# Other homes for the output gates and other prices for side work in a one-core fp32 decoder layer

## The chip, the cores and the metric

The kernel is one program on one core of a Trainium2 chip. The metric is the device time of one execution in microseconds (us), as the median over several. The engines in the profile are PE (TensorE matmuls), PEld (its weight loads, which overlap), DVE (VectorE), ACT (ScalarE), POOL (GpSimd) and SP (which starts most transfers).

## The reference, cut to what matters

One layer of a hybrid decoder for 256 prompt tokens and 8 sample tokens (264 columns), width 2048, all in fp32. Everything of the first part comes out of one projection of the normalized input:

```python
z = rmsnorm(x, g_mix) @ w_in
xr, conv_new = causal_conv(z[RGX], conv_buf, conv_w, conv_b)      # RG-LRU, 1024 channels
log_a = -8 * sigmoid(block_diag(xr, w_rg_a)) * softplus(-lam)
a = exp(log_a); bx = sqrt(1 - exp(2 * log_a)) * (sigmoid(block_diag(xr, w_rg_x)) * xr)
h_rg = scan(h = a * h + bx)
y_rg = rmsnorm(h_rg * gelu(z[RGG]), g_rg_out)
h_ml, C, n, m = mlstm(z[Q], z[K], z[V], z[I], log_sigmoid(z[F]), C0, n0, m0)   # 4 heads
y_ml = rmsnorm_per_head(h_ml, g_ml_out) * sigmoid(z[O])           # 1024 channels
x = x + concat(y_rg, y_ml) @ w_out
x = x + cross_attention(rmsnorm(x, g_xa), memory) ; x = x + swiglu(rmsnorm(x, g_ffn))
return rmsnorm(x, g_final), all new states
```

The change lies in all that comes up to `w_out`, and in the norm of the memory tokens (`mem_gen`) that is done beside it. The cross attention, the SwiGLU layer and the final norm are as they were.

## The kernel before, in words

**Steps.** Activations lie transposed, channels on the 128 partitions and 264 tokens in a row. A projection is cut into blocks of 128 output channels, and each block is a *step*, an entry of the list `steps`, with index `i`. An fp32 product is made of three matmuls on fp32r parts (`mm3`): high x high, high x low, low x high. A step has 16 chunks of 128 input channels, so 48 matmuls, and it has two halves of 8 chunks, 24 matmuls each, because its weights come in two pieces of 128 x 1024.

A piece is loaded into a `raw` buffer (5 of them) by a transfer from SP, and is split into a `w` buffer (4 of them) by `split_half`: ScalarE copies the high part to fp32r, VectorE subtracts it to get the low part. A `w` buffer comes free when the half step that reads it has ended. The right operands lie in `B` buffers (26) as pairs of high and low parts. Results go to PSUM banks, `mm` for steps (4) and `ax` for all else (4).

The steps in order: 0 to 3 are the RG-LRU input blocks 0 to 3, done together chunk by chunk in four banks (`pe_first`), with pieces that are split in parts as `x` arrives; 4 to 7 are the blocks 4 to 7 of it; 8 the input and forget gates (`pe_if`); 9 to 16 q and k; 17 to 24 v; 25 to 32 the RG-LRU output gates (`rgg`); 33 to 40 the mLSTM output gates (`evac_o`); 41 to 56 the output projection `w_out`, whose right operand `ry(c)` is y_rg for chunks 0 to 7 and y_ml for 8 to 15; then the queries, keys and values of the cross attention, and so on.

**The norm of x.** Steps 0 to 40 use x times the gain, without the norm. The factor `rstd` of each token is multiplied in when a result is taken out of PSUM. `norm_x` makes it: sums of squares `acc_x` (one ScalarE square and one VectorE sum per chunk), column sums by matmul, an rsqrt of 12 small VectorE operations on 128x3 columns (`c`), and `spread`, three matmuls that lay the columns out over all partitions. Until it is done no step's result leaves PSUM.

**Side work.** What is not a step is written as Python generators: `norm_x`, `rg_gen` (exponentials, roots and scans of the RG-LRU), `ml_prompt` and `ml_sample` (the mLSTM; in the second the sample states `B` are scaled by `bcs` and multiplied into `nums`), `ml_norm` (per head: squares and sums into a B buffer, four matmuls with `pick`, an rsqrt on 128x12 columns, four spreads, eight products), `mem_gen` (squares and sums over the memory tokens in `lt`, then the norm). After each step the loop calls `pump`, which lets them run on in order of their priority while two virtual clocks, one for VectorE and one for ScalarE, are behind the virtual clock of TensorE. The clocks advance by the prices of `price_dve`, `price_act` and `price_pe`. `finish` runs side work without regard to the clocks until a condition holds; a step's `need` names generators that must be finished before it.

The results of a step wait in `pend` and are taken out at the next step, at high priority. `rg_gen` must be done before step 25 (`need=("rg",)`). `evac_o(j)` takes out an output gate, and makes the product with the mLSTM output at once; for that it calls `finish` until `ml_norm` has that head (`ml["nn"]`), so the whole of `ml_norm` is forced at step 33's evacuation.

The order that comes out of the Python is not the order on the engines: a scheduler of the language orders each engine's instructions by a time model and by priority. `in_order()` and `manual_schedule` keep the written order for the named engines within them.

The main loop's lines that the text speaks of:

```python
        if i == 5:
            finish(lambda: fn.done)
            st["rg"] = side(rg_gen(), 0)
        for q in need:
            if q in st:
                finish(lambda: st[q].done)
```

Of the kernel before, what the change touches and what calls it, by code (L numbers as in the profile page):

```python
# [17 lines left out]
P = 128  # L18
D = 2048
KC = D // P  # L20
T = 256
# [40 lines left out]


def price_dve(name, n, a, k):
# [3 lines left out]
    return 0.07 + n * (0.00052 if fast else 0.0066 if name == "reciprocal" else 0.00104)  # L68


def price_act(name, n, a, k):
    return 0.12 + n * 0.00083

# [7 lines left out]
def layer_kernel(ctx: ExitStack, tc, xT, memT, vec, wrg, w_in, w_out, w_q, w_k, w_v, w_o,  # L81
# [120 lines left out]
    def split_first(i, h):  # L202
# [9 lines left out]
        splits[i, h] = (wh, wl)  # L212

    def wrows(w, i):

        w = w[:, WO: WO + 8 * N].rearrange("p (c n) -> p c n", n=N)
        return w[:, :, 0: P], w[:, :, P: 2 * P]
# [97 lines left out]

    warm(12)
    onesr = const.tile([P, P], F32R, name="onesr")
# [294 lines left out]
    def evac_if(ps):  # L612
        R = Arr(7)
        ml["R"] = R
        li, u, a, b = (R(j)[0:4] for j in range(4))
        act.activation(halves(a), unturn(ps[64:68, :N]), AF.Copy)
        act.activation(halves(b), unturn(ps[96:100, :N]), AF.Copy)
        dve.tensor_add(halves(li), unturn(ps[0:4, :N]), halves(a))
        dve.tensor_add(halves(u), unturn(ps[32:36, :N]), halves(b))
        dve.tensor_mul(li, li, rstd[0:4, :])  # L620
        dve.tensor_mul(u, u, rstd[0:4, :])
        dve.tensor_scalar(li, li, V("bi")[0:4], None, op0=OP.add)
        dve.tensor_scalar(u, u, V("bf")[0:4], None, op0=OP.add)
        ml["gates"] = side(ml_gates(), 1)
# [6 lines left out]
    def ml_gates():  # L631
# [32 lines left out]
        for h in range(H):  # L664
            pe.matmul(ps[:, h * 16: h * 16 + 16], ident[0:4, h: h + 1].to_broadcast([4, P]), x16,
                      start=True, stop=True)
        i4 = ident[0:4, 0:4]
        for j in range(2):
            pe.transpose(ps[:, 64 + 4 * j: 68 + 4 * j], g[:, j * P: j * P + P], i4)
        for j, w0 in enumerate(WIN):  # L670
            pe.transpose(ps[:, 72 + 4 * j: 76 + 4 * j], b[:, w0: w0 + P], i4)
        act.activation(bcs, ps[:, 0:64].rearrange("p (h j) -> p h j", j=16), AF.Copy)
# [30 lines left out]
    def ml_prompt():  # L703
# [11 lines left out]
        R = ml["R"]  # L715
        M = R(6)[0:4, :T]
        for h in range(H):
            sel = ident[0:4, h: h + 1].to_broadcast([4, P])
            bc = bank("ax")
# [138 lines left out]
    def ml_norm():  # L858
# [35 lines left out]
        for h in range(H):  # L894
# [112 lines left out]
    def mem_gen():  # L1007
# [14 lines left out]
        for c in range(KC):  # L1022
# [3 lines left out]
            split(m[:, :T], m[:, T:], x, V("g_mem", c))  # L1026
            yield 0.7

    def ry(c):
# [304 lines left out]

    load_x(sp, 0, 1)
    for c in range(4):
        load_first(0, c)
    for i in range(1, 3):
        for c in range(0, 4, 2):
# [3 lines left out]
        if i == 1:  # L1343
            sp.dma_start(vecs[:, 16:], vec[:, 16:])
    with tc.high_priority(), in_order():
        act.dma_start(vecs[:, 0:16], vec[:, 0:16])
        load_x(act, 1, 2)
        load_x(act, 2, 4)
        act.activation(warm_act, ones[:, 0:1], AF.Square)
        split_half(0, 0)  # L1350
        split_half(0, 1)

    pend = []
    for i, (src, cols, pef, evf, need) in enumerate(steps):
# [19 lines left out]
        if 1 <= i < 4:  # L1374
            with tc.issue_after(st["split"].ins):
                for c in range(4 * i if i > 1 else 0, 4 * i + 4):
                    sumsq(acc_x, xres[:, c, :], c == 0)
        if i == 3:
            fn = side(norm_x(), -1)
        if evf is not None:  # L1380
# [9 lines left out]
        if i == 24:  # L1390
            ml["ng"] = side(ml_norm(), 6)
        if i == 40:
# [114 lines left out]
```

## Time and profile before

| | |
|---|---|
| median of 3 runs | 1467.48 us (1466.98 to 1468.0) |
| profiled execution, its own time | 1467.75 us |
| its span | 1466.0 us |
| PE busy | 1446.3 us (99%) |
| DVE busy | 1063.4 us (73%) |
| ACT busy | 783.8 us (53%) |
| POOL busy | 126.1 us (9%) |
| moved by transfers | 326.01 MB, mean 222 GB/s |
| mean granted TensorE clock | 0.995 |

The span is what the profile covers; the execution's own time is 1.75 us longer. All recorded instructions are made by one helper, so nearly every row names L60, and an instruction is told by its tiles: `w<-raw` is the split of a weight piece, `mm<-B,w` a step's matmul, `ax<-...` one of the side work. In timelines and groups the buffers' numbers are left out. A timeline row has start, length, engine, line, operation, out<-in, shapes, count, and in brackets the idle time ahead of it with what ended it. A row of a table of stretches has the stretch, its length, the busy time and count of PE, PEld, DVE, ACT and POOL, then the granted clock as a share of full speed, the share of the transfer engines and GB/s. A row of a group has, behind the bar, busy time and mean nanoseconds, and behind the second bar the idle time ahead of its instructions and what ended most of it.

### The profile page before, as it was taken

The page shows a single profiled execution, that of the slowest core. Times are in us where ns is not written, and L with a number is a line of the kernel's source. Part 1 is how long each engine was busy: PE and PEld are TensorE (multiplying, and loading weights), DVE is VectorE, ACT ScalarE, POOL GpSimd, SP SyncE. Part 2 cuts the span into 40 slices and gives each one's busy share as a digit, 9 for nine tenths or more (in the row PEclk, how much of TensorE's full clock was granted, in tenths as well). Part 3 has the DMA queues.
Part 4 walks back from the last instruction along what each step waited for, and adds up shares of the span by engine and source line. Part 5 has one row for each costly group of instructions (what it writes and reads, how often), then busy time and mean ns, then how long its engine had stood idle before and what let it go on. Part 6 is the DMA issues. An engine that isn't in the chain of part 4 may idle for free.

```text
span 1466.0 us, 30118 instructions
## 1 busy us (share of the span) xinstructions
PE 1446.3 (99%) x12052; PEld 1418.9 (97%) x12052; DVE 1063.4 (73%) x2050; ACT 783.8 (53%) x1254; POOL 126.1 (9%) x193
## 2 busy tenths in 40 slices
PE   8999999999999999999999999999999999999997
PEld 8998899999999999999999999999999999999997
DVE  7986888898799999986676656555566555566564
ACT  7565675675466666665544444344444434444463
POOL 0001110000124344320000000000000000000000
PEclk9999999999999999999999999999999999999999
DMA  9554986556799989955655555655555565555563
GB/s 280 206 187 156 309 300 230 186 189 216 246 364 335 341 280 343 346 201 186 198 192 194 194 198 193 199 192 197 196 193 201 189 200 193 196 196 193 173 193 111
DMA packets 99756, 326.01 MB, mean 222 GB/s; under 512 B 10944, under 2 KB 19824, under 8 KB 99616
## 3 DMA queue, kind: packets, MB, share of 16 engines
q1 hardware_dynamic: 83472, 269.57, 54.8%
q0 software_dynamic: 15136, 53.16, 10.1%
q8 instruction: 94, 1.54, 0.4%
q10 hardware_dynamic: 1008, 1.36, 0.3%
q14 instruction: 46, 0.38, 0.1%
HBM read 312.78 MB, written 11.28 MB: 221 GB/s over the span
## 4 chain that ended last, share of the span: by engine, by line
PE 51%; issue 42%; DVE 3%; DMA 2%; ACT 2%; POOL 0%; POOLq 0%; SPq 0%; DVEq 0%; ACTq 0%
PE mm L60 48%; PE ax L60 4%; DVE B L60 2%; DVE w L60 1%; DMA raw<-w_in 1%; ACT B L60 1%; ACT w L60 0%; DMA B<-scr 0%; DMA o_sc<-B 0%; ACT L60 0%; DMA scr<-lt 0%; DVE acc_x L60 0%; POOL B L1399 0%; ACT t L60 0%; POOL B L830 0%
## 5 line engine op out<-in xcount | busy, mean ns | idle before, releaser
L60 PE MATMUL mm<-B,w 128*128 128x264 f32 (+1 forms) x10960 | 1286.6, 279 | 7.4 <-ACT w L60 2.8
L60 PEld LDWEIGHTS mm<-B,w 128*128 128x128 f32 x10960 | 1264.8, 190 | 18.1 <-DVE w L60 3.5
L60 DVE TENSOR_TENSOR w<-raw,w 128x1024 fp32r<-128x1024 f32 (+1 forms) x522 | 624.4, 1198 | 300.5 <-ACT w L60 299.5
L60 ACT ACTIVATE w<-raw 128x1024 fp32r<-128x1024 f32 (+1 forms) x522 | 536.3, 1029 | 549.9 <-PE mm L60 383.0
L60 PE MATMUL mm<-w,B 128*128 128x512 f32 x384 | 86.5, 380 | 0.0
L60 PEld LDWEIGHTS mm<-w,B 128*128 128x128 f32 x384 | 70.7, 189 | 9.4
L1399 POOL TENSOR_TENSOR B<-B,rstd 128x264 f32<-128x264 f32 x4 | 2.8, 740 | 803.4 <-ACT rstd L60 803.4
L60 DVE TENSOR_TENSOR t<-mm,rstd 128x264 f32<-128x264 f32 x104 | 44.8, 431 | 28.4 <-PE mm L60 28.3
L60 DVE SCALAR_TENSOR_TENSOR B<-B,dw 128x256 f32<-128x256 f32 x128 | 53.7, 473 | 2.8 <-ACT dw L60 2.6
L60 DVE TENSOR_TENSOR xres<-xres,mm 128x264 f32<-128x264 f32 (+1 forms) x81 | 34.3, 424 | 27.6 <-PE mm L60 27.5
L60 DVE SCALAR_TENSOR_TENSOR dw<-B,qsm,dw 128x256 f32<-128x256 f32 x96 | 48.7, 512 | 0.8
L60 PE MATMUL ax<-B,B 128*128 128x256 f32 (+3 forms) x288 | 47.2, 305 | 0.8 <-DVE B L60 0.7
L1083 POOL TENSOR_TENSOR ds<-dw,ds 128x256 fp32r<-128x256 f32 x32 | 36.0, 1126 | 105.2 <-ACT ds L60 105.1
L60 PEld LDWEIGHTS ax<-B,B 128*128 128x128 f32 x288 | 39.5, 191 | 4.5 <-DVE B L60 1.4
L60 ACT ACTIVATE B<-xres,vecs 128x264 fp32r<-128x264 f32 (+1 forms) x64 | 32.1, 502 | 4.8 <-DVE xres L60 4.0
L60 ACT ACTIVATE t<-xres 128x264 f32<-128x264 f32 (+1 forms) x61 | 23.9, 409 | 15.9 <-DVE xres L60 15.9
L1072 POOL DMA_DIRECT2D B<-kcT x32 | 17.3, 542 | 142.4 <-DVE B L60 129.5
L60 ACT ACTIVATE dw<-B,qsm 128x256 f32<-128x256 f32 x32 | 16.3, 509 | 19.9 <-issue 9.9
L60 DVE SCALAR_TENSOR_TENSOR B<-xres,vecs,B 128x264 fp32r<-128x264 f32 x48 | 23.4, 488 | 3.5 <-ACT B L60 3.5
L60 DVE TENSOR_TENSOR acc_x<-acc_x,t 128x264 f32<-128x264 f32 x59 | 25.1, 426 | 1.0 <-ACT t L60 0.5
L60 ACT ACTIVATE t<-t 128x264 f32<-128x264 f32 (+1 forms) x61 | 24.7, 406 | 1.5 <-DVE t L60 1.5
L60 ACT ACTIVATE B<-t 128x264 fp32r<-128x264 f32 (+1 forms) x60 | 24.1, 409 | 1.5 <-DVE t L60 1.5
(168 smaller groups left out, 673.3 us busy)
## 6 DMA issues: line engine op xcount, KB each, us to landing
raw<-w_gu SPq DMA_DIRECT2D x176, 512.0 KB, 3.9
raw<-w_d SPq DMA_DIRECT2D x80, 512.0 KB, 4.2
raw<-w_in SPq DMA_DIRECT2D x74, 512.0 KB, 4.7
raw<-w_out SPq DMA_DIRECT2D x32, 512.0 KB, 4.5
B<-kcT POOLq DMA_DIRECT2D x32, 512.0 KB, 9.3
raw<-w_q SPq DMA_DIRECT2D x32, 512.0 KB, 5.1
B<-vcT POOLq DMA_DIRECT2D x32, 512.0 KB, 10.8
raw<-w_k SPq DMA_DIRECT2D x32, 512.0 KB, 5.3
```

Source lines behind the costliest of these rows:

```text
L60: return f(*a, **k)
L1072: pool_e.dma_start(kc, kcT[h, b])
L1083: pool_e.tensor_sub(ws[:, 1], acc, ws[:, 0].bitcast(F32))
L1399: e.tensor_mul(st["y"](c), st["y"](c), r)
```

## The change

1. *Start.* 8 warm-up matmuls instead of 12; the first weight piece is the first transfer of SP, the first chunk of x goes to ScalarE's queue, the next three behind weight pieces on SP.
2. *Squares.* In step 1 those of chunks 0 to 7 are made one by one, as before. Chunks 8 to 15 are done at step 3 by two squares of 128x1056 and four sums (`last_squares`), in place of eight of each.
3. *First norm.* `norm_x` is no longer forced at step 5. PE's order is as written in steps 4 to 6, and the two parts of `norm_x` are written into it: the column sums in step 5 after chunk 8, the spread in step 6 after chunk 2. The results of steps 3 to 6 leave PSUM from step 7 on, and `rg_gen` begins at 7 instead of 5.
4. *Prices.* `price_dve` and `price_act` have higher fixed parts and rates for some kinds (the scan twice the rate) until step 41; from there on they are the old ones.
5. *Output gates.* `evac_o` makes the sigmoid and leaves it in a B array `z`. `ml_norm`, written on by a loop over eight blocks, multiplies and splits. `ml_norm` has to be done before step 41 (`need` "ng"), and nothing asks for it before. Step 40's results leave PSUM ahead of that.
6. *Gate rows.* Two tiles of the gates are zeroed on GpSimd, and the matmuls that select and transpose gate rows use all 128 rows in place of 4.
7. `mem_gen`'s last loop gives way every second chunk.

The diff, cut:

```diff
 def price_dve(name, n, a, k):
...
+    rate = {"reciprocal": 0.0066, "tensor_tensor_scan": 0.00208}.get(name, 0.00052 if fast else 0.00104)
+    fixed = 0.21 if name == "scalar_tensor_tensor" else 0.15
+    return fixed + n * rate + (0.08 if "accum_out" in k else 0.0)
 def price_act(name, n, a, k):
...
+    return (0.27 if by_column else 0.18) + n * 0.00085 + (0.2 if "accum_out" in k else 0.0)
+    def last_squares():
+        a, b = (B([P, BW])[:, 0: 4 * N] for _ in range(2))
+        for t, q in ((a, 2), (b, 3)):
+            act.activation(t, xres[:, 4 * q: 4 * q + 4, :].rearrange("p c n -> p (c n)"), AF.Square)
+        dve.tensor_add(a, a, b)
...
+        dve.tensor_add(acc_x, acc_x, a[:, 0: N])
-    warm(12)
+    warm(8)
     def evac_if(ps):
+        for q in range(2):
+            pool_e.memset(R.tile(q), 0.0)
     def ml_norm():
...
-            ml["nn"] = h + 1
+        for j in range(8):
+            while ml.get("zn", 0) <= j:
+                yield STEP
+            if j == 0:
+                st["yml"] = HL(8)
+            z = ml["z"](j)
+            dve.tensor_mul(z, z, hh(j))
+            split(*st["yml"](j), z, V("g_ml", j))
+            yield 0.8
     def evac_o(j):
         def f(ps):
-            z = tmp()
+            if j == 0:
+                ml["z"] = Arr(8)
+            z = ml["z"](j)
             dve.tensor_mul(halves(z), unturn(ps[:, :N]), halves(rstd))
             act.activation(z, z, AF.Sigmoid)
-            if j == 0:
-                st["yml"] = HL(8)
-            finish(lambda: ml.get("nn", 0) > j // 2)
-            dve.tensor_mul(z, z, hT["t"](j))
-            split(*st["yml"](j), z, V("g_ml", j))
+            ml["zn"] = j + 1
     def proj(src, rhs, evac, cols=2048, n=N, need=()):
+                if (i, c) in ((5, 9), (6, 3)):
+                    with tc.high_priority():
+                        st["rstd_x"].run(lambda: True)
     for m in range(KC):
         proj(w_out[m], ry, residual(m, "g_xa", "xa", norm_wide),
-             need=("rgout",) if m == 0 else ())
+             need=("rgout", "ng") if m == 0 else ())
...
-        if i == 5:
-            finish(lambda: fn.done)
+        if i == 7:
             st["rg"] = side(rg_gen(), 0)
+        if "ng" in need:
+            with tc.high_priority(300):
+                for e, x in pend:
+                    e(x)
+            pend = []
-        if i != 4:
+        if not 4 <= i < 7:
+        if i == 4:
+            kept.enter_context(tc.manual_schedule(engines={mybir.EngineType.PE}))
         ps = pef(i)
+        if i == 6:
+            kept.close()
-            ml["ng"] = side(ml_norm(), 6)
+            st["ng"] = side(ml_norm(), 6)
+        if i == 41:
+            PACE["full"] = False
```

**Where the instructions stand.** In the rows that follow a name's first number tells apart tiles of one kind, and `x2` says that two alike stand together.

TensorE before, in step 33's and 34's x projections (`mm_383`, `mm_396`): `ax_378` is the bank into which `ml_norm` sums its squares with `pick`.

```order
L60 MATMUL mm_383_2987<-B_37_360,w_374_2913 128x264
L60 MATMUL ax_378_2969<-B_358_2810,pick_91 4x264
L60 MATMUL mm_383_2987<-B_36_359,w_374_2913 128x264
L60 MATMUL ax_378_2969<-B_358_2810,pick_91 4x264
L60 MATMUL mm_383_2987<-B_36_359,w_374_2913 128x264
L60 MATMUL ax_378_2969<-B_358_2810,pick_91 4x264
L60 MATMUL mm_383_2987<-B_37_360,w_374_2913 128x264
...
L60 MATMUL mm_396_3080<-B_13_150,w_381_2981 128x264
L60 MATMUL mm_396_3080<-B_14_151,w_381_2981 128x264
L60 MATMUL ax_378_2969<-B_358_2810,pick_91 4x264
```

TensorE after, at the output projection: `mm_489`, `mm_496`, `mm_502` and `mm_508` are the banks of steps 41 to 44, `w_494` and `w_500` the first pieces of 43 and 44, `w_391`, `w_488`, `w_495` and `w_501` the second pieces of 41 to 44, `B_359` and `B_371` parts of y_rg, `B_471` of y_ml. Of the `w` buffers one is `w_494`, then `w_500`, then `w_501`.

```order
L60 MATMUL mm_502_3936<-B_371_3250,w_494_3865 128x264
L60 MATMUL mm_508_4001<-B_359_3114,w_500_3930 128x264
...
L60 MATMUL mm_508_4001<-B_371_3250,w_500_3930 128x264
L60 MATMUL ax_443_3637<-B_433_3602,pick_87 4x264 x4
...
L60 MATMUL ax_467_3717<-ident_69,c_447_3649 128x128 x2
...
L60 MATMUL mm_489_3806<-B_471_3742,w_391_3412 128x264
...
L60 MATMUL mm_496_3871<-B_471_3742,w_488_3803 128x264
...
L60 MATMUL mm_502_3936<-B_471_3742,w_495_3868 128x264
...
L60 MATMUL mm_508_4001<-B_471_3742,w_501_3933 128x264
```

The norm's matmuls moved from between x projections to behind the first halves of four steps of the output projection, and ahead of those steps' second halves.

VectorE before, at the same norm: the split of `w_395`, RG-LRU gate work (`acc_rg`, `B_178`) and the first operations of the rsqrt chain in `c_388`.

```order
L60 TENSOR_TENSOR w_395_3077<-raw_377_2967,w_395_3077 128x8x128
L60 TENSOR_TENSOR acc_rg_102<-acc_rg_102,t_372_2907 128x264
L60 TENSOR_TENSOR B_178_1652<-B_178_1652,t_379_2974 128x264
L60 TENSOR_TENSOR t_392_3067<-mm_383_2987,rstd_98 128x264
L60 TENSOR_TENSOR acc_rg_102<-acc_rg_102,t_380_2978 128x264
L60 SCALAR_TENSOR_TENSOR c_388_3046<-ax_386_3041,c_388_3046 128x3x4
L60 TENSOR_TENSOR w_405_3164<-raw_384_3036,w_405_3164 128x8x128
L60 TENSOR_SCALAR c_388_3046<-c_388_3046 128x12
```

VectorE after: from the split of `w_501` on, `ml_sample`'s state updates (`B_415`, `nums`), the sums of `ml_norm` in `B_433`, sums of `mem_gen` in `lt_450`, the chain in `c_446` to `c_449`, and the products with the spread factors.

```order
L60 TENSOR_TENSOR w_501_3933<-raw_491_3857,w_501_3933 128x8x128
L60 SCALAR_TENSOR_TENSOR B_415_3539<-B_415_3539,bcs_99,t_427_3580 128x256
L60 SCALAR_TENSOR_TENSOR t_428_3584,nums_105<-B_415_3539,B_416_3540 128x128 x2
...
L60 TENSOR_TENSOR B_433_3602<-B_433_3602,t_435_3608 128x264
...
L60 TENSOR_TENSOR lt_450_3669<-lt_450_3669,t_451_3671 128x256
...
L60 SCALAR_TENSOR_TENSOR c_446_3648<-ax_444_3643,c_446_3648 128x3x4
L60 TENSOR_TENSOR lt_450_3669<-lt_450_3669,t_459_3695 128x256
...
L60 TENSOR_TENSOR B_263_2454<-B_263_2454,ax_467_3717 128x264 x2
...
L60 SCALAR_TENSOR_TENSOR B_472_3743<-B_343_2972,vecs_91,B_471_3742 128x264
```

The chain of the norm, between weight splits before, stands after without one from `w_501` to the parts of y_ml, and it shares VectorE with state updates and memory sums.

VectorE after, at the first norm: the end of the rsqrt chain (`c_59`, `c_57`), the split of `w_63`, and the first results that leave PSUM (`B_68`); TensorE's spread reads `c_57` and stands behind nine matmuls of step 6, where it stood behind 42 before.

```order
L60 SCALAR_TENSOR_TENSOR c_59_601<-c_59_601,c_56_595 128x3
L60 TENSOR_TENSOR w_63_639<-raw_51_555,w_63_639 128x8x128
L60 SCALAR_TENSOR_TENSOR c_57_596<-c_59_601,c_57_596 128x3
L60 TENSOR_TENSOR B_68_701<-ax_2_106,rstd_94 128x132
L60 TENSOR_TENSOR B_68_701<-ax_2_106,rstd_94 128x124
```

The last operation of the chain has moved behind a weight split.

More of the change, by code (lines that the diff above doesn't have):

```diff
@@ L61, in __getattr__ @@
         return call
+PACE = {"full": True}
 def price_dve(name, n, a, k):
@@ L664, in ml_gates @@
         for h in range(H):
-            pe.matmul(ps[:, h * 16: h * 16 + 16], ident[0:4, h: h + 1].to_broadcast([4, P]), x16,
+            pe.matmul(ps[:, h * 16: h * 16 + 16], ident[:, h: h + 1].to_broadcast([P, P]), R(2)[:, 0:16],
                       start=True, stop=True)
[L667 to L671, printed above, removed]
+        for o, x, at in ((64, R(5), WIN[:2]), (72, R(4), WIN)):
+            for j, w0 in enumerate(at):
+                pe.matmul(ps[:, o + 4 * j: o + 4 * j + 4], x[:, w0: w0 + P], ident[:, 0:4], start=True, stop=True)
         act.activation(bcs, ps[:, 0:64].rearrange("p (h j) -> p h j", j=16), AF.Copy)
@@ L715, in ml_prompt @@
         R = ml["R"]
-        M = R(6)[0:4, :T]
+        M = R(6)[:, :T]
         for h in range(H):
-            sel = ident[0:4, h: h + 1].to_broadcast([4, P])
+            sel = ident[:, h: h + 1].to_broadcast([P, P])
             bc = bank("ax")
@@ L1027, in mem_gen @@
             yield 0.7
+            if c % 2:
+                yield STEP
     def ry(c):
@@ L1333, in load_x @@
         e.dma_start(xres[:, lo:hi, :], xT[:, lo:hi, :])
-    load_x(sp, 0, 1)
     for c in range(4):
         load_first(0, c)
+        if c == 0:
+            load_x(sp, 1, 2)
+        elif c == 1:
+            load_x(sp, 2, 4)
     for i in range(1, 3):
@@ L1345, in layer_kernel @@
     with tc.high_priority(), in_order():
+        load_x(act, 0, 1)
         act.dma_start(vecs[:, 0:16], vec[:, 0:16])
-        load_x(act, 1, 2)
-        load_x(act, 2, 4)
         act.activation(warm_act, ones[:, 0:1], AF.Square)
@@ L1351, in layer_kernel @@
         split_half(0, 1)
+    PACE["full"] = True
     pend = []
+    kept = ExitStack()
     for i, (src, cols, pef, evf, need) in enumerate(steps):
@@ L1372, in layer_kernel @@
             split_half(i + LS, 1)
+        if i == 4:
+            kept.enter_context(tc.manual_schedule(engines={mybir.EngineType.PE}))
         ps = pef(i)
-        if 1 <= i < 4:
+        if i == 6:
+            kept.close()
+        if i == 1:
             with tc.issue_after(st["split"].ins):
-                for c in range(4 * i if i > 1 else 0, 4 * i + 4):
+                for c in range(8):
                     sumsq(acc_x, xres[:, c, :], c == 0)
         if i == 3:
-            fn = side(norm_x(), -1)
+            with tc.issue_after(st["split"].ins), tc.high_priority():
+                last_squares()
+            st["rstd_x"] = Gen(norm_x())
         if evf is not None:
```

9 lines of the change are left out of this document (7 added, 2 removed).

## The prediction

> **What bounds the kernel now.** I read the page first, then the table of stretches, then TensorE's timeline around its waits, then the granted clock there.
>
> ```profile
> span 1466.0 us, 30118 instructions
> PE 1446.3 (99%) x12052; PEld 1418.9 (97%) x12052; DVE 1063.4 (73%) x2050; ACT 783.8 (53%) x1254; POOL 126.1 (9%) x193
> ...
> 260.00:280.00 20.00, 20.00 (x180) 20.00 (x179) 18.49 (x34) 13.38 (x23) 0.00 (x0) 1.00 0.57 193
> ```
>
> TensorE is the bound. The last row is a stretch at its limit: 180 matmuls in 20.00 us, 0.111 us each, so a half step (24 matmuls) takes 2.7 us and a step 5.3. No such matmul is added or removed, so the change can win only time in which TensorE stands still or runs slowly. In its timeline that time is in brackets, with what ended it:
>
> ```profile
> 7.61 0.94 PE L60 MATMUL ax<-B,w 128*128 128x264 f32 x6 [1.00 <-ACT w L60]
> 24.74 0.60 PE L60 MATMUL ax<-B,w 128*128 128x264 f32 x3 [0.58 <-ACT w L60]
> 32.04 1.17 PE L60 MATMUL mm<-B,w 128*128 128x264 f32 x8 [0.95 <-DVE w L60]
> 51.64 11.35 PE L60 MATMUL mm<-B,w 128*128 128x264 f32 x84 [2.02 <-DVE B L60]
> 117.95 0.49 PE L60 MATMUL mm<-B,w 128*128 128x264 f32 x2 [1.86 <-ACT w L60]
> 122.25 9.98 PE L60 MATMUL mm<-B,w 128*128 128x264 f32 x67 [1.17 <-DVE w L60]
> 177.98 1.57 PE L60 MATMUL ax<-B,B 128*128 128x256 f32 x8 [0.71 <-DVE B L60]
> 338.97 0.49 PE L60 MATMUL mm<-B,w 128*128 128x264 f32 x2 [0.97 <-ACT w L60]
> ```
>
> After two of them the granted clock (third column from the right) falls:
>
> ```profile
> 50.00:55.00 5.00, 3.36 (x15) 3.39 (x16) 5.00 (x22) 1.76 (x11) 0.00 (x0) 0.66 0.58 201
> 120.00:125.00 5.00, 3.83 (x17) 3.42 (x17) 5.00 (x9) 2.93 (x7) 0.00 (x0) 0.50 0.30 100
> 125.00:130.00 5.00, 5.00 (x39) 5.00 (x38) 4.86 (x13) 1.72 (x4) 0.58 (x2) 0.83 0.75 238
> ```
>
> That costs 0.34 x 5 = 1.7 us after the first norm, and (0.50 + 0.17) x 5 = 3.35 us at 120, less half of the 1.17 idle in it: 2.8 us. So there is to be won: 0.58 + 0.95 us (steps 3 and 4), 2.02 + 1.7 = 3.7 (first norm), 1.86 + 1.17 + 2.8 = 5.8 (RG-LRU burst), 0.71 and 0.97, together 12.7 us, and a part of the first 7.61.
>
> **What the change wins, part by part.**
>
> ```profile
> 1.12 5.49 PE L60 MATMUL mm<-ones 128*128 128x128 f32 x24 [1.12 <-DVE ones L60]
> 20.01 0.63 ACT L60 ACTIVATE w<-raw 128x512 fp32r<-128x512 f32 x1 [1.23 <-DMA raw<-w_in]
> 28.24 1.35 ACT L60 ACTIVATE t<-xres 128x264 f32<-128x264 f32 x4
> 29.35 1.50 DVE L60 TENSOR_TENSOR acc_x<-acc_x,t 128x264 f32<-128x264 f32 x3
> ```
>
> *Start and squares.* Eight warm-up matmuls instead of twelve end at 1.12 + 5.49 x 8/12 = 4.8 us, so the first real matmul could come up to 2.8 us earlier, the first weight piece now leading its queue. But at 20.01 ScalarE waits for a weight load in the middle of a saturated stretch, and an earlier TensorE would wait there instead. What surely goes is the work ahead of step 4's splits: four squares (1.35 us on ScalarE) and three sums (1.50 on VectorE), now two wide squares behind those splits. I take 1.8 us (0.6 with only the 0.95 and less than nothing earlier, 2.8 at best).
>
> *First norm.* The 3.7 us go, for the evacuations now have step 7's start as their deadline. New is that TensorE's order is pinned: the spread stands after 9 matmuls of step 6, and on VectorE the last operation of the rsqrt chain stands behind a split whose buffer comes free only as step 6 begins.
>
> ```profile
> L60 ACT ACTIVATE w<-raw 128x1024 fp32r<-128x1024 f32 x90 | 94.5, 1054 | 69.6 <-PE mm L60 51.5 <-issue 13.8 <-ACT t L60 3.0
> L60 DVE TENSOR_TENSOR w<-raw,w 128x1024 fp32r<-128x1024 f32 x89 | 107.8, 1217 | 17.8 <-ACT w L60 17.2
> ```
>
> 1.05 + 1.22 + 0.17 for the last small operation = 2.4 us, against 9 x 0.111 = 1.0 of cover: a wait of 1.4 (0 to 2.0). Half a chance of a slow clock behind it is 0.8. Seven evacuations and their convolutions now crowd steps 7 to 9 on VectorE; I take 1.0 for it (0 to 2.5, the row of 2.02 being the nearest). Net 3.7 - 3.2 = 0.5 us (-2.0 to 3.7). [...]
>
> *RG-LRU burst.* With the higher prices the exponentials and roots come in two batches with weight splits between, but step 25 still forces the end. The worst place is between the two splits of step 24 on VectorE:
>
> ```profile
> L60 DVE TENSOR_TENSOR B<-B,B 128x264 f32<-128x264 f32 x16 | 6.4, 418 | 3.0 <-ACT B L60 3.0
> L60 DVE TENSOR_TENSOR_SCAN B<-B,B 128x256 f32<-128x256 f32 x8 | 5.4, 678 | 0.0
> ```
>
> 8 products and 5 scans, less the 0.08 by which neighbours overlap, 8 x 0.34 + 5 x 0.60, with an evacuation and three small ones 6.3 us, and the split 1.2: 7.5 us against 2.7 of matmuls and a lead of 3.4 (the roots on ScalarE hold it there): 1.4 us wait (0 to 3.3 with a slow clock). 5.8 - 1.4 = 4.4 us.
>
> The 0.71 and 0.97 waits go, 1.7 us (0.5 to 1.7): at both places VectorE has less to do than before. Zeroed gate rows and full-height selections keep the number of matmuls, and an idle GpSimd zeroes them: nothing. Gains: 1.8 + 0.5 + 4.4 + 1.7 = 8.4 us (1.6 to 14.0).
>
> **What it loses: the output projection.** Before, step 33's gate forced the mLSTM norm to its end while projections of x were left to run. The norm's matmuls stand between full streams and nothing waits:
>
> ```profile
> 224.98 0.61 PE L60 MATMUL ax<-B,pick 128*4 128x264 f32 x2
> 230.93 0.73 PE L60 MATMUL ax<-ident,lt 128*128 128x4 f32 x6
> 231.51 9.59 PE L60 MATMUL mm<-B,w 128*128 128x264 f32 x83
> 240.93 2.74 PE L60 MATMUL ax<-ident,c 128*128 128x128 f32 x24
> ```
>
> Now nothing forces it before step 41, whose operands it makes. TensorE runs the first halves of steps 41 to 44, which need only the RG-LRU half; then all it has left hangs on the norm. Of four w buffers three hold second halves, and one passes from w_494 to w_500 to w_501. VectorE is in order, so all it does for the norm stands behind w_501's split, and that split behind TensorE's end with w_500. The prices:
>
> ```profile
> L60 DVE SCALAR_TENSOR_TENSOR B<-B,bcs,t 128x256 f32<-128x256 f32 x32 | 15.3, 478 | 3.2 <-ACT t L60 3.1
> L60 DVE SCALAR_TENSOR_TENSOR t<-B,B 128x128 f32<-128x128 f32 x64 | 18.3, 288 | 2.7 <-DMA B<-scr 1.4
> L60 DVE TENSOR_TENSOR lt<-lt,t 128x256 f32<-128x256 f32 x15 | 6.3, 420 | 0.3
> L60 DVE SCALAR_TENSOR_TENSOR c<-c,c 128x12 f32<-128x12 f32 x6 | 1.0, 169 | 0.1
> 242.73 1.44 DVE L60 TENSOR_TENSOR B<-B,ax 128x264 f32<-128x264 f32 x4
> ```
>
> 1. w_500's split begins at the end of w_494: 1.05 + 1.22, less 0.4 of matmuls that need only its upper part: 1.9 us (1.0 to 2.3).
> 2. w_501's split, 2.1 us after w_500. Then VectorE: 3 x 0.478 + 6 x 0.288 (state updates), 4 x 0.42, 15 x 0.42 (sums for the memory norm that stand in between), 14 x 0.17, 6 x 0.42 and the first low part 0.48: 16.6 us at mean lengths. But four take 1.44, not 1.68, so neighbours overlap by 0.08: 12.7 us. Four trips to TensorE or ScalarE inside the chain (0.2 to 0.7 each) add 1.0. So 13.7 (12.7 to 18).
> 3. Off comes what TensorE does meanwhile: 4 x 0.45 + 0.6 + 2.7 + 0.45 = 5.5 us of the norm's own matmuls, fp32, which it did before too. Idle: 2.1 + 13.7 - 5.5 = 10.3 us.
> 4. Restart at half clock, as in the rows at 120 (5.1 us slow, so 2.2 lost here), and step 45's splits, whose buffers come free only as the four second halves end: 0.8.
>
> 1.9 + 10.3 + 2.2 + 0.8 = 15.2 us (11 to 21). A longer wait would be hidden only by x projections, and none is left.
>
> **Sum.** 15.2 - 8.4 = 6.8 us slower. The profiled execution took 1467.75 us, 0.27 above the median of 1467.48: 1474.5 us.
>
> **The rivals.** *Faster.* TensorE restarts early: ScalarE's roots and the state updates are done sooner, so VectorE passes its 49 operations at the dense 0.36 spacing with no trip added, the clock stays at 1.00, and the waits at the spread and the scans stay hidden. Then 11 us are lost and 13.5 won: 1465. It decides from the point at which the loss falls below the gain less 2.9 us. For it speaks that ScalarE is half idle; against it that the chain passes TensorE four times.
>
> *The two cancel.* Gains near 13 against a loss near 14, or 9 against 10: 1465 to 1470, within 0.2% (2.9 us), about what a measurement of this kernel can tell from no change.
>
> *A longer stop.* TensorE's clock stays at half through the second halves (up to 3.4 more), the memory sums wait for ScalarE's squares in front of the norm (2), and the first norm wins nothing (2): 1482.
>
> *The change does not do what it says.* Side work "priced as traced" may only be late, so that a forced end takes the place of a burst: this is in my forecast at step 41, and at step 25 it would give back 3 of the 4.4 us: 1477.
>
> **How the numbers follow.** Slower by the stop at step 41, as summed, with the step 25 case: 0.64. Longer stop 0.17, cancel 0.12, faster 0.07. Slower is 0.64 + 0.17 = 0.81. The sum's ends are 1467.7 + 11 - 14.0 = 1465 and 1467.7 + 21 - 1.6 = 1487; both need every term at one end, so I give 1467 to 1483, which leaves out the faster case, a part of the cancelling one and the last of the long stop.
>
> **What would show it.** Right: one wait of TensorE of about 8 us or in pieces a little above 10 together near 265 to 285 us, ended by VectorE or ScalarE writing B, the clock at half behind it; no wait near 117; first matmul near 5 to 6 us; a wait of 1 to 2 us before the spread. Wrong: TensorE at 20.00 of 20.00 in every stretch from 240 to 300, as in the row above, or a longest wait under 4 us after 200.

## The result, and the profile after

The changed kernel takes 1481.19 us (median of 4 runs, 1480.73 to 1482.34) against 1467.24 before (4 runs, one more than in the table of before): a ratio of 1.0093, 95% interval 1.008 to 1.0105, or 13.9 us slower. The profiled execution took 1481.5 us.

The head of the page of after, where TensorE's busy time is nearly as it was (1447.2 us for 1446.3) and the span 13.8 us longer:

```profile
span 1479.8 us, 30118 instructions
PE 1447.2 (98%) x12049; PEld 1418.9 (96%) x12049; DVE 1067.4 (72%) x2046; ACT 792.0 (54%) x1254; POOL 125.1 (8%) x195
```

TensorE's timeline of after, the rows with a wait that matter (start, length, what, and in brackets the idle time ahead and what ended it):

```profile
5.19 1.69 PE L60 MATMUL ax<-B,w 128*128 128x264 f32 x6 [0.28 <-ACT w L60]
44.77 0.81 PE L60 MATMUL ax<-ident,c 128*128 128x128 f32 x6 [1.89 <-DVE c L60]
152.52 2.74 PE L60 MATMUL mm<-B,w 128*128 128x264 f32 x22 [0.73 <-DVE w L60]
270.84 0.49 PE L60 MATMUL mm<-B,w 128*128 128x264 f32 x2 [1.15 <-ACT w L60]
272.10 2.74 PE L60 MATMUL mm<-B,w 128*128 128x264 f32 x22 [0.77 <-DVE w L60]
280.79 3.41 PE L60 MATMUL ax<-B,pick 128*4 128x264 f32 x8 [5.95 <-DVE B L60]
284.73 0.83 PE L60 MATMUL ax<-ident,lt 128*128 128x4 f32 x6 [0.53 <-ACT lt L60]
290.88 5.29 PE L60 MATMUL ax<-ident,c 128*128 128x128 f32 x24 [5.32 <-DVE c L60]
480.18 4.63 PE L60 MATMUL mm<-B,w 128*128 128x256 f32 x27 [1.19 <-DVE w L60]
500.77 0.38 PE L60 MATMUL ax<-ds,onesr 128*128 128x256 f32 x1 [0.99 <-POOL ds L1114]
```

The waits of 0.95, 2.02, 1.86, 1.17, 0.71 and 0.97 us are gone; the one of 0.58 in step 3 is now 0.80, at 24.27. The stop that the prediction put near 265 to 285 us is there, from 269.7 to 290.9. The last two rows are in the cross attention, where before had no wait longer than 0.1 us. In the table of stretches of after the third column from the right is the granted clock: it is low in the stop, and once more at 502.

```profile
275.00:280.00 5.00, 0.00 (x0) 0.00 (x0) 4.10 (x16) 3.87 (x10) 0.00 (x0) 0.70 0.90 354
285.00:290.00 5.00, 0.56 (x6) 0.47 (x5) 4.68 (x19) 1.54 (x4) 0.00 (x0) 0.72 0.00 0
290.00:295.00 5.00, 4.12 (x19) 4.12 (x20) 3.32 (x13) 0.92 (x2) 0.00 (x0) 0.50 0.00 0
500.00:520.00 20.00, 18.52 (x87) 16.13 (x88) 19.03 (x39) 12.81 (x21) 3.84 (x5) 0.91 0.64 218
```

To lay the time to places I add up, for each stretch of steps, TensorE's idle time and its busy time at half clock times one half: the *lost time*. For after the span less the lost time is 1437.8 us, for before 1439.0, so on the whole it accounts for nearly all. The first column holds the time until the clock is first granted in full (at 7.27 us in before, 7.31 in after); the column differs between kernels with one and the same start (3.4 us in e9, 6.1 in e4), and a profiled run can lie 3 us off its median (e2 above, e10 below); the columns behind the first are what to compare. In us, with the experiments (e1 to e12) that follow:

| steps | 0-2 | 3-7 | 8-24 | 25-40 | 41-47 | 48-72 | 73-108 | end | sum |
|---|---|---|---|---|---|---|---|---|---|
| before | 4.9 | 5.3 | 5.9 | 0.7 | 0.0 | 1.3 | 0.0 | 8.9 | 27.0 |
| **after** | 4.4 | 2.7 | 0.7 | 0.0 | 19.0 | 0.0 | 6.7 | 8.5 | 42.0 |
| e1 debt forgiven | 3.9 | 2.9 | 0.7 | 0.0 | 21.3 | 0.6 | 0.0 | 8.8 | 38.3 |
| e2 old prices | 4.9 | 2.7 | 7.6 | 10.7 | 0.0 | 0.4 | 0.1 | 8.5 | 34.9 |
| e3 dear to step 24 | 4.0 | 2.7 | 0.7 | 0.0 | 16.4 | 1.2 | 0.0 | 9.1 | 34.1 |
| e4 gates as before | 6.1 | 1.6 | 0.7 | 22.4 | 0.0 | 0.0 | 12.0 | 8.5 | 51.3 |
| e5 prices alone | 6.4 | 3.0 | 2.6 | 22.3 | 0.0 | 0.9 | 12.6 | 8.9 | 56.8 |
| e6 gates alone | 7.0 | 4.7 | 7.6 | 0.7 | 0.0 | 3.9 | 0.1 | 8.9 | 33.0 |
| e7 start, squares, norm | 4.3 | 3.1 | 8.0 | 6.5 | 0.0 | 1.2 | 0.1 | 9.1 | 32.1 |
| e8 candidate | 4.0 | 5.6 | 0.7 | 13.9 | 5.4 | 1.4 | 0.1 | 8.8 | 39.8 |
| e9 prices less 0.08 | 3.4 | 3.1 | 1.8 | 1.3 | 3.6 | 0.5 | 0.0 | 8.9 | 22.5 |
| e10 with credit | 5.1 | 2.7 | 4.3 | 10.0 | 0.0 | 0.8 | 2.9 | 9.2 | 35.0 |
| e11 memory sums later | 4.2 | 2.7 | 0.7 | 0.0 | 18.6 | 1.9 | 0.2 | 8.7 | 37.1 |
| e12 spread later | 3.7 | 1.2 | 1.8 | 1.5 | 5.2 | 0.5 | 0.1 | 8.9 | 22.9 |

So the change won 16.8 - 7.8 = 9.0 us in the first four columns and 1.3 in steps 48 to 72, lost 19.0 in the stop, and lost 6.7 at a place of which the prediction says nothing.

### The profile page after: what moved, and what is told of

It is laid out like the page before. It is cut to its first block, busy times and chain, and to the rows that moved or that the text cites. A ratio compares the mean times of both kernels' runs of the same rounds, so it can differ in the third digit from the quotient of the medians.

```text
span 1479.8 us, 30118 instructions
## 1 busy us (share of the span) xinstructions
PE 1447.2 (98%) x12049; PEld 1418.9 (96%) x12049; DVE 1067.4 (72%) x2046; ACT 792.0 (54%) x1254; POOL 125.1 (8%) x195
## 4 chain that ended last, share of the span: by engine, by line
PE 56%; DVE 0%; ACT 0%; POOL 0%; issue 0%; DVEq 0%; POOLq 0%; ACTq 0%
PE mm L60 56%; PE ax L60 1%; DVE B L60 0%; POOL ds L1114 0%; DVE c L60 0%; DVEq L1531 0%; ACT ds L60 0%; ACT dw L60 0%; ACT t L60 0%; DVE xres L60 0%; ACT c L60 0%; ACTq L60 0%; POOLq L1165 0%; POOLq L1114 0%
## 5 line engine op out<-in xcount | busy, mean ns | idle before, releaser
L60 DVE TENSOR_TENSOR t<-mm,rstd 128x264 f32<-128x264 f32 x96 | 41.5, 433 | 29.5 <-PE mm L60 29.4
L60 DVE SCALAR_TENSOR_TENSOR dw<-B,qsm,dw 128x256 f32<-128x256 f32 x96 | 52.2, 548 | 1.9 <-ACT dw L60 1.4
L1114 POOL TENSOR_TENSOR ds<-dw,ds 128x256 fp32r<-128x256 f32 x32 | 32.8, 1026 | 183.6 <-ACT ds L60 183.4
L60 ACT ACTIVATE dw<-ax,dw 128x256 f32<-128x256 f32 x32 | 15.0, 470 | 21.2 <-DVE dw L60 20.7
L60 ACT ACTIVATE ds<-dw 128x256 fp32r<-128x256 f32 x32 | 13.2, 413 | 21.1 <-DVE dw L60 20.9
```

The lines of the kernel that those rows point to most:

```text
L60: return f(*a, **k)
L1114: pool_e.tensor_sub(ws[:, 1], acc, ws[:, 0].bitcast(F32))
```

## The experiments

Ratios are to the kernel before on the same chip (median 1469.3 to 1469.9 there, single runs 1464.9 to 1472.6), with their 95% interval. The changed kernel itself was not timed again there, so it is compared with the experiments by the ratios. Parts 6 and 7 of the change were not tested alone.

**What the attention pays for.** While the program is built, the loop's virtual clocks can be printed. After step 41 of the changed kernel VectorE's stands at 297.8 and TensorE's at 256.3, since the forced end of `ml_norm` is booked on it. Until TensorE's has caught up, about step 60, `pump` lets `mem_gen` do next to nothing; then the decoding attention (`dec_k`, `dec_v`) goes first, and what is left of `mem_gen` is forced at step 73. In before it was written out by step 51. e1 takes the debt away:

```diff
                 finish(lambda: st[q].done)
+        if "ng" in need:
+            dve.clock = act.clock = pe.clock
```

> The changed kernel, with one line more: once the forced end of ml_norm ahead of step 41 is written, the virtual clocks of VectorE and ScalarE are set back to TensorE's (by the loop's own numbers 297.8 and 274.5 against 256.3 after step 41). Theory A, the debt: mem_gen stands still from step 41 to about step 61 because the forced work stays booked on VectorE's clock, is then outranked by the decoding attention, and is forced at step 73; that crowds the cross attention and is the 9.2 us that the changed kernel loses after step 72. Then this run is 9 us faster, about 1472, with the stop between 269 and 291 us as it was (about 13.7 us of idle). Rival B, chance: the attention's order is another one because the scheduler's time model moved by some us; then paying off the debt changes little: 1478 to 1484.

Measured 1475.01 us, 1.0043 (1.0028 to 1.0057), between the two forecasts. The stretches of e1 in the cross attention decide: TensorE is at its full 20.00, where after has 18.14, 18.87 and 18.52. The stop is still there, 21.3 us for 19.0 in the table:

```profile
460.00:480.00 20.00, 20.00 (x140) 18.82 (x139) 19.93 (x57) 12.54 (x22) 9.60 (x16) 1.00 0.96 354
480.00:500.00 20.00, 20.00 (x106) 17.86 (x105) 19.46 (x40) 12.23 (x21) 10.42 (x13) 1.00 1.00 389
500.00:520.00 20.00, 20.00 (x119) 18.24 (x118) 18.78 (x48) 12.63 (x22) 6.90 (x8) 1.00 0.84 299
```

The whole way from the first matmul over the memory tokens (`mm<-B,w`, 128x256) to the end is 8.8 us longer in after than in before and as long in e1 as in before, with the same 8293 matmuls. The rows are of before, after and e1:

```profile
457.76:1466.00 1008.24, 999.36 (x8293) 981.80 (x8291) 675.32 (x1105) 497.54 (x720) 79.23 (x105) 1.00 0.63 214
462.78:1479.80 1017.02, 1003.53 (x8293) 983.06 (x8291) 680.90 (x1117) 499.12 (x727) 75.41 (x104) 1.00 0.61 211
465.24:1473.40 1008.16, 999.36 (x8293) 981.74 (x8291) 674.71 (x1105) 497.08 (x720) 80.89 (x105) 1.00 0.63 214
```

Theory A holds, and chance doesn't: the loss in the attention is the forced work of step 41, handed on as a debt to a generator that had no part in it.

**Prices or buffers.** e2 puts the old prices back (`PACE["full"] = False` in both places), e3 ends the higher ones early (`if i == 24:` instead of 41), e4 puts `evac_o`, the end of `ml_norm` and the `need` back as they were before and keeps the prices.

> The changed kernel with the old prices throughout. Theory A, the prices: with dear prices less side work passes per step, so ml_sample and ml_norm are late at step 41; with the old ones all of ml_norm but the products with the last gates is written by step 36, the stop of TensorE at 269 to 291 us is gone, mem_gen ends by step 53 and the 9.2 us in the attention are gone too, while the RG-LRU burst comes back (up to 5.8 us): 1481.2 - 14 - 9 + 5.8 = 1464, 1460 to 1467. Rival B, the gate buffers: ml_norm has nothing that asks for it before step 41, so it is late at any price: a stop of 8 us or more stays, 1470 to 1480.

Measured 1469.88 us, 1.0006 (0.9993 to 1.0019). No stop at step 41 and nothing lost in the attention, as theory A has it; but the burst is back, and a wait of 3.57 us at 230 for a result to leave PSUM, with a half clock behind it (26 matmuls in 6.06 us, 0.233 each for 0.111). 1464 was too good, and the rival's stop is not there either.

> The changed kernel with the higher prices until step 24 instead of step 41. Theory A (late ml_norm by the prices): no burst near 117, no stop at step 41, mem_gen done before step 73: 1481.2 - 14.1 - 9.2 = 1458, 1455 to 1462. Rival B (the buffers, and the loss of the forced end at step 33): a stop of 8 us or more at step 41 stays, 1468 to 1480.

Measured 1472.29 us, 1.0022 (1.0011 to 1.0033), as the rival had it. The attention is clean, but a stop of 10.55 us stands at step 41, now for y_rg. Theory A in the form "late since step 24" falls. I take it that the side work was behind by then already; e3 alone does not show it.

> The changed kernel with the output gates as before: evac_o multiplies at once and forces ml_norm at step 33's evacuation; the higher prices stay. Theory A: ml_norm is just as late and the same work is forced at step 34, where six steps of x projections are left to run, so the stop shrinks to some 3 to 6 us; the debt is the same (258.4 against 217.6 after step 34), mem_gen is again forced at step 73, and the attention's 9 us stay: about 1472, 1467 to 1476. Rival B, the buffers are the cause: stop and attention excess go, 1456 to 1462.

Measured 1489.6 us, 1.0142 (1.0118 to 1.0165), the wrong way for both. The forced end at step 34 stops TensorE for 19.65 us in one piece:

```profile
264.46 2.80 PE L60 MATMUL ax<-B,pick 128*4 128x264 f32 x6 [19.65 <-DVE B L60]
267.19 3.62 PE L60 MATMUL mm<-B,w 128*128 128x264 f32 x18
```

The x projections that should have covered it did not: the matmuls with `pick` stand ahead of the next projection in TensorE's row, and no matmul of the projection ran ahead of them. When the wait ends, six of them run, and then 18 of the projection. So the buffers do not cause the loss: with the dear prices they are what makes it smaller.

**Each part alone on the kernel before.** e5 has the prices alone, e6 the gate buffers alone, e7 start, squares and first norm; e8 is a candidate of start, squares, buffers, and the higher prices until step 14.

> The kernel before, with the higher prices until step 41 and nothing else of the change. Theory A (the dear prices make the side work late): the RG-LRU burst near 117 to 127 us goes (5 us won), ml_sample and ml_norm are not written by step 33 and are forced there (259.3 on VectorE's clock against 218.5 on TensorE's after step 34), with a stop of about 20 us as in the run with the gates as before, and the memory norm comes late too: 1467.5 - 5 + 20 + 3 = 1485, 1480 to 1492. Rival B (the prices alone do no harm; it takes the gate buffers or the moved first norm): 1461 to 1466.

Measured 1499.89 us, 1.0205 (1.0189 to 1.022): worse than the whole change, and 15 us above the forecast. In e4 and e5, which leave nearly the same debt as the change (40.8 us for 41.5), steps 73 to 108 lose 12.0 and 12.6 us in the table; in the runs without it that is at most 0.2, but for 2.9 in e10, for which I have no reason. TensorE's timeline of e5 at the forced end:

```profile
272.06 2.80 PE L60 MATMUL ax<-B,pick 128*4 128x264 f32 x6 [19.74 <-DVE B L60]
```

> The kernel before, with the output gates in buffers and ml_norm needed at step 41, old prices. Theory A: by the loop's clocks ml_norm is written by step 33 but for the products with the gates, as before, so nothing is late at step 41 and no stop over 2 us is there: 1467, within 3 us of before. Rival B (the buffers make ml_norm late whatever the prices): a stop at step 41 of 8 us or more, 1474 to 1482.

Measured 1471.97 us, 1.0007 (0.9995 to 1.0019): no difference, and no wait at step 41.

> The kernel before, with the new start, the batched squares and the first norm in blocks 6 and 7, and nothing else. Lost time up to step 7's end was 10.2 us before and 7.1 in the changed kernel. If that gain is kept: 1464. If the side work that then starts two steps later (rg_gen at step 7, not 5) makes ml_norm late at step 33 (forced there for some 5 us by the loop's clocks), the gain is given back: a stop of 2 to 6 us near 225 us, 1466 to 1470. I hold the second for likelier, since the run with old prices throughout had a wait of 3.6 us there.

Measured 1471.3 us, 1.0009 (1.0 to 1.0019): 2.8 us won by step 7, and given back (8.0 for 5.9 in the burst, 6.5 for 0.7 at steps 25 to 40, where a wait of 3.58 us is back at 228).

> A candidate: the kernel before with the new start, the batched squares, the gate buffers, and the higher prices only until step 14; first norm as before. By theory A the burst is spread (rg_gen ends at step 22, not 17), ml_norm is written by step 40 without being forced, so no stop at 41: 1467.5 - 1.5 - 5 + 1 = 1462, 1459 to 1466. If VectorE has simply too little time left before step 41 once the burst is spread (as the run with the higher prices until step 24 suggests, with its stop of 10.6 us), a stop of 5 to 12 us near 265 us: 1468 to 1475.

Measured 1478.83 us, 1.0057 (1.004 to 1.0074), above both forecasts: waits of 3.21 us at 174, 4.64 at 228 and 2.38 at 283, nowhere a single large stop.

**What the price should have been.** In the trace of before four products of 0.42 us take 1.44 (at 242.73), so they start (1.44 - 0.42) / 3 = 0.34 apart: the traced length of each reaches about 0.08 into its neighbour's. No run shows why. For the state updates of `ml_sample` VectorE's timeline of after has the spacing itself, one scaling and two products with their sums:

```profile
273.03 0.48 DVE L60 SCALAR_TENSOR_TENSOR B<-B,bcs,t 128x256 f32<-128x256 f32 x1
273.54 0.29 DVE L60 SCALAR_TENSOR_TENSOR t<-B,B 128x128 f32<-128x128 f32 x1
273.76 0.08 DVE L60 DVE_READ_ACCUMULATOR t<-B,B 128x1 f32 x1
273.88 0.29 DVE L60 SCALAR_TENSOR_TENSOR t<-B,B 128x128 f32<-128x128 f32 x1
274.10 0.08 DVE L60 DVE_READ_ACCUMULATOR t<-B,B 128x1 f32 x1
274.10 0.48 DVE L60 SCALAR_TENSOR_TENSOR B<-B,bcs,t 128x256 f32<-128x256 f32 x1
...
275.97 1.23 DVE L60 TENSOR_TENSOR w<-raw,w 128x1024 fp32r<-128x1024 f32 x1 [0.73 <-ACT w L60]
```

From scaling to scaling it is 274.10 - 273.03 = 1.07 us. The old prices make it 0.336 + 2 x 0.203 = 0.74, the higher ones 0.476 + 2 x 0.423 = 1.32, and those less 0.08 for each instruction 1.08. With the lower prices TensorE waited in small pieces (3.57 us at 230 in e2, 3.58 at 228 in e7); I read that as more work than VectorE could do there. With the higher ones VectorE was left idle early (19.5 us in the rows of after below), and the rest was forced at the end. e9 takes the last:

```diff
-    fixed = 0.21 if name == "scalar_tensor_tensor" else 0.15
+    fixed = 0.13 if name == "scalar_tensor_tensor" else 0.07
-    return (0.27 if by_column else 0.18) + n * 0.00085 + (0.2 if "accum_out" in k else 0.0)
+    return (0.19 if by_column else 0.10) + n * 0.00085 + (0.2 if "accum_out" in k else 0.0)
```

> The changed kernel with each of the higher prices lower by 0.08 us, the time by which neighbours on VectorE and ScalarE overlap in the trace (four products of 0.42 take 1.44). Theory A2: a traced length is not what an instruction takes of its engine when others stand beside it, so prices as traced charge too much, the loop hands VectorE too little side work (it is busy 0.84 and 0.68 of the time from 60 to 120 and 120 to 180 us), and what is left over is forced at step 41. By the loop's clocks ml_norm is then written by step 40, its last products at 41, with no debt, and mem_gen ends by step 54. Then no forced end, no loss in the attention, and a stop at 41 of 5 us or less: 1481 - 9 - 9 = 1463, 1460 to 1468. Rival B2: VectorE cannot do the work before step 41 in any case once TensorE runs ahead by the 18 us won before: the stop is as in the run with the higher prices until step 24 (10 us and a half clock): 1470 to 1475.

Measured 1463.1 us, 0.9955 (0.994 to 0.9969): 6 us faster than before and, with e12, the best of these kernels. It is one value: no price beside it was tried, and e10, which differs from e9 only in a credit of 3 us, is 15 us slower. So how much of the gain is the right price, and how much an order that happens to fit, is not shown. In the table of stretches the fourth group is VectorE's busy time; after, first, leaves it idle for 19.5 us from 120 to 180 and has not a moment left from 240 to 260:

```profile
120.00:180.00 60.00, 59.27 (x514) 58.61 (x514) 40.54 (x74) 44.18 (x74) 4.88 (x9) 1.00 0.53 173
240.00:260.00 20.00, 20.00 (x180) 20.00 (x180) 20.00 (x54) 16.39 (x33) 6.03 (x12) 1.00 0.99 341
```

The same of e9:

```profile
120.00:180.00 60.00, 56.95 (x480) 55.35 (x480) 44.15 (x103) 37.85 (x69) 7.52 (x14) 1.00 0.69 230
240.00:260.00 20.00, 20.00 (x178) 19.93 (x177) 18.88 (x53) 15.19 (x32) 3.49 (x7) 1.00 0.71 235
```

What is left of the stop in e9's TensorE timeline are the waits for weight splits and three short ones:

```profile
278.10 0.49 PE L60 MATMUL mm<-B,w 128*128 128x264 f32 x2 [1.15 <-ACT w L60]
279.54 2.52 PE L60 MATMUL mm<-B,w 128*128 128x264 f32 x20 [0.95 <-DVE w L60]
286.28 1.50 PE L60 MATMUL mm<-B,w 128*128 128x264 f32 x11 [0.98 <-DVE B L60]
288.05 1.28 PE L60 MATMUL mm<-B,w 128*128 128x264 f32 x9 [0.26 <-DVE B L60]
289.52 5.67 PE L60 MATMUL mm<-B,w 128*128 128x264 f32 x48 [0.20 <-DVE w L60]
```

e10 is e9 with clocks set to TensorE's less 3 us at a step's start (`max(dve.clock, now - 3.0)` and the like).

> As the run with the prices less 0.08 us, and the clocks of VectorE and ScalarE are set to TensorE's less 3 us at a step's start instead of to TensorE's itself, so that up to 3 us of idle time is kept and can be spent on side work later. By the loop's clocks rg_gen ends at step 18 and ml_norm stands by step 32 but for the products with the gates. Theory A2: no stop at step 41 at all, but a part of the burst near 125 us is back (3 to 6 us): 1460 to 1467. Rival B2: the work is denser than VectorE can do, so TensorE waits in several places near 125, 175 and 230 us as in the run with old prices: 1468 to 1473.

Measured 1478.61 us, 1.0064 (1.0046 to 1.0081), worse than either case: 4.3 us lost in steps 8 to 24, 10.0 in 25 to 40 (waits of 1.80 at 207 and 3.36 at 224). I read it as a burst again, of idle time saved up and spent at once; no further run tests that.

**Two terms of the prediction.** e11 is e1 with `mem_gen` started at step 46 instead of 40.

> The changed kernel with the clocks set back after the forced end at step 41, as in the first run, and mem_gen started at step 46 instead of 40. It takes away the sums over memory tokens that stood between the norm's operations on VectorE while TensorE waited. The prediction's term: 15 sums at 0.36 = 5.4 us of the stop. If they lay on the path that ends the stop, idle time from 265 to 295 us goes from 13.5 to about 8 to 9 us and the kernel is 5 to 6 us faster than the first run's 1475: 1469, 1467 to 1471. Rival: ScalarE or the transfers of sample states end the chain, and the sums only filled VectorE's gaps: 1473 to 1476.

Measured 1475.07 us, 1.0037 (1.0024 to 1.005): as e1, and as the rival had it. TensorE's timeline of e11 in the stop:

```profile
282.11 3.68 PE L60 MATMUL ax<-B,pick 128*4 128x264 f32 x8 [5.95 <-DVE B L60]
290.70 5.29 PE L60 MATMUL ax<-ident,c 128*128 128x128 f32 x24 [2.94 <-DVE c L60]
```

The wait ahead of the spread is 2.94 for 5.09 us in e1, so of the 5.4 us of memory sums some 2.2 lay on the path. A part came back elsewhere (1.9 us in steps 48 to 72, for 0.6 in e1).

e12 is e9 with the spread of the first norm after 24 matmuls of step 6, `(6, 8)` for `(6, 3)`.

> The best kernel so far (the changed one with its higher prices less 0.08 us), and the spread of the first norm in step 6 after chunk 7 instead of chunk 2: 24 matmuls, 2.7 us, ahead of it instead of nine, 1.0. In all runs with the spread after nine matmuls TensorE waited 1.56 us (1.89 in one) ahead of it for VectorE's last operation of the rsqrt chain. If that wait is only a matter of cover, it goes whole, for 15 more matmuls are 1.67 us: 1463.1 - 1.5 = 1461.6, 1460.5 to 1462.5. Rival: the results that leave PSUM after the spread are then late for step 7 to 9, and TensorE waits there instead: 1463 to 1464.5.

Measured 1462.75 us, 0.9954 (0.9941 to 0.9968). The wait is gone and no other in its place, 1.9 us in the table; but in the profiled run the clock fell at the same two waits that e9 has at step 44 (granted 0.78 from 275 to 280 us and 0.88 from 280 to 285, for 1.00 in e9), which cost 1.6. The medians of e9 and e12 can't be told apart.

## Why the prediction was right, and where it was not

It held in sign and range (1481.2 in 1467 to 1483), with 6.8 us forecast and 13.9 measured. The stop was forecast rightly, its cause was not, and a second loss of 8.8 us was not in the sum. That the range holds the time all the same is luck, for its upper end was made of other terms. The kernel without that loss, e1, has the ratio 1.0043, which is 1473.5 on the scale of the 1467.24, against the 1474.5 of the sum.

- *Start and squares, first norm, burst, the small waits.* Right, but for sizes. First matmul at 5.19 us (5 to 6 forecast), wait of 0.95 gone, wait ahead of the spread 1.89 (1.4 forecast), clock at 1.00 behind it (0.8 was charged), no wait of TensorE in steps 7 to 9 (1.0 was charged for a crowd on VectorE). The scan case cost 0.73 at 152.52 (1.4). By the table steps 0 to 40 won 9.0 us and 48 to 72 another 1.3: 10.3 where 8.4 was forecast.
- *The stop at step 41.* Place, engine and chain as forecast. The splits: 1.15 + 0.77 = 1.9 us, the term as it stood. Step 45's splits cost no wait (0.8 was charged); one of 0.49 came later, at 322.87. The chain: 5.95 + 0.53 + 5.32 = 11.8 idle for 10.3. VectorE's timeline of after from the last split to the spread, cut:

```profile
277.11 0.48 DVE L60 SCALAR_TENSOR_TENSOR B<-B,bcs,t 128x256 f32<-128x256 f32 x1
...
280.31 1.46 DVE L60 TENSOR_TENSOR B<-B,t 128x264 f32<-128x264 f32 x4
281.69 4.12 DVE L60 TENSOR_TENSOR lt<-lt,t 128x256 f32<-128x256 f32 x8
285.72 0.17 DVE L60 SCALAR_TENSOR_TENSOR c<-ax,c 128x12 f32<-128x12 f32 x1
...
290.25 0.37 DVE L60 SCALAR_TENSOR_TENSOR c<-c,c 128x12 f32<-128x12 f32 x2
290.66 0.17 DVE L60 TENSOR_TENSOR c<-c,c 128x12 f32<-128x12 f32 x1
```

  It takes 13.7 us, where the forecast's terms up to there make 10.2 and at most 1.0 for trips. Two terms were mis-sized. The three state updates took 3.2 us: I had 3 x 0.478 + 6 x 0.288 less 0.08 of overlap for each, 2.4, but a read of the accumulator stands behind each product, and a group takes 1.07, not 0.81. And the memory sums, the small operations and the trip over TensorE between them took 9.1, for 6.4 and at most 1.0 for trips. There e11 shows the sums to be worth 2.2 of the 5.1 that I charged; the rest was too low, for the small operations stand 0.2 us apart (290.25 to 290.66 for two), where I had 0.09. TensorE's own matmuls in the wait took 4.2 us for 2.4, partly at half clock, and the work behind the spread, 2.4 us in the sum, held up nothing, so that only 1.5 us more idle time is left. Slow clock 4.8 us for 2.2, since the clock fell twice (0.50 from 277.0 to 283.8 and from 287.2 to 297.4, with 9.56 us of busy time; the rows at 120 that the sum names would have given 2.8). Together 19.0 for 15.2.
- *Up to step 72 the sum was near, and partly by luck.* The first matmul over the memory tokens starts at 457.76 us in before and at 462.78 in after, 5.0 later for 6.8 forecast. Decoding's first row of `ds` on GpSimd says the same, in before and then in after:

```profile
392.94 1.05 POOL L1083 TENSOR_TENSOR ds<-dw,ds 128x256 fp32r<-128x256 f32 x1 [25.97 <-ACT ds L60]
```

```profile
397.97 1.06 POOL L1114 TENSOR_TENSOR ds<-dw,ds 128x256 fp32r<-128x256 f32 x1 [95.25 <-ACT ds L60]
```

  By the table the loss up to there is 19.0 - 10.3 = 8.7. The difference of 3.7 us is busy time of TensorE that is shorter in after; no term of the sum holds it, and I have no row that lays it to a place. The other 8.8 us come behind (the rows at 457.76 and 462.78): 6.7 are lost time in the attention, and some 2.5 are busy time of TensorE that grew there; the end gave 0.4 back.
- *What failed.* "Now nothing forces it before step 41" was taken for the cause. e6 and e5 show that it isn't: the buffers alone cost nothing, the prices alone 30 us. Before, the loop had `ml_norm` written out after step 32 by its own pace, so step 33's evacuation had nothing to force, and what the prediction says of that (and the description of the kernel) is wrong for this program. In the sum I had set the prices down as the cure of the burst alone, and did not ask what a higher price does to all the work behind it; only a rival has the thought.
- *What was not looked at.* The sum ended at step 46. A forced end has a second cost in a loop that keeps accounts: it is owed, and the next generator pays (e1, 8.8 us).

The rival "the change does not do what it says" had the right thought ("side work priced as traced may only be late") with the wrong place and price. The half chance of a slow clock behind the first norm's wait was an estimate, and the clock stayed full there, behind 1.89 us. It fell elsewhere: the 0.70 in the row at 275 is 3.0 us at half clock, so it fell at 277.0, when TensorE had been idle for 2.2 us (its last matmul ended at 274.84); and in e12 it fell at two waits of together 2.10 us (1.15 and 0.95 in e9, where it did not).

## What to carry to other kernels

Work that is paced by a table of prices did better here with the time by which instructions stand apart when the engine is busy than with their traced length (0.9955 in e9 for 1.0093): too low a price gave many small waits (e2, e7), and too high a one left the engine idle early (19.5 us from 120 to 180 in after) and forced the rest at the worst place. Check a price against a group that repeats (here 1.07 us), and the pace against the engine's busy time per stretch: idle in one stretch and full in a later one is the sign. Where work is forced, follow what its account does to the next in line; the largest surprise of this change lay 200 us behind its cause.

## What the runs showed of the hardware

- Traced lengths overlapped where instructions stand back to back: by about 0.08 us on VectorE (before, at 242.73: four products of 128x264, 0.42 long and 0.34 apart) and 0.09 on ScalarE (after, at 280.85: eleven squares of 0.40 in 3.47, so 0.31 apart). It was not so for every instruction: the eight memory sums at 281.69 in after, each of which adds to the tile that the one before wrote, stand (4.12 - 0.42) / 7 = 0.53 apart, though ScalarE's squares for them, 0.31 apart from 280.85 on, are ready. That the shared tile is the reason was not tested. A price of the length less 0.08, as in e9, is too low for them.
- Behind each product of the state updates, which has a sum as second output, stands a separate read of 0.08 us (after, at 273.76 and 274.10). In the group of these updates five rows of together 1.22 us take 1.07.
- The granted clock, once it had been full, was half in before for 3.41 us from 51.64 and 6.83 from 119.91, in after for 6.83 from 276.96, 10.24 from 287.20 and 3.41 from 502.24, and in both from some 5 us before the end (1461.3 and 1475.0). Idle time of 2.02 us was followed by it once (before, up to 51.64), 1.89 us was not (after, up to 44.77), and two waits of together 2.1 us were in e12 and not in e9. Runs of one program differed in it: the mean granted clock of e12's six runs is 0.997 or 0.998, and one spell of 3.41 us at half clock in 1461.5 us is worth 0.0012.
